# The low part of every other up-projection weight tile is formed by an adding transfer instead of a VectorE subtraction

## The chip, the cores and the metric

The kernel runs on one core of a Trainium2 chip. The core has TensorE (PE, with its weight loads as PEld), VectorE (DVE), ScalarE (ACT), GpSimd (POOL) and SyncE (SP), which only issues transfers here. Sixteen DMA engines move data between device memory and the on-chip memory. The metric is device time in microseconds (us) of one execution; lower is better.

## The reference, cut to what matters

One decoder layer over 256 tokens of width 2048: a normed residual goes through one q/k/v projection for two groups of heads (a softmax group and a stick-breaking group), each group's output is normed, one output projection and a residual follow, and then a squared-ReLU MLP of inner width 8192, a residual and a last norm. Everything is float32. The part that the change touches is the product with `w_up`:

```python
h = rmsnorm(x, mlp_norm_g[l])                       # (1, 256, 2048)
u = jnp.einsum('bsd,df->bsf', h, w_up[l])           # w_up: 2048 x 8192
x = x + jnp.einsum('bsf,fd->bsd', jnp.square(jax.nn.relu(u)), w_down[l])
return rmsnorm(x, final_norm_g)
```

## The kernel before, in words

**Items.** All weights (50.3 million float32 numbers, some 201 MB) are read once, as a stream of 1 MiB items (`items`, lines 81 to 97). An item is 512 rows by 512 columns, held as 128 partitions x 4 k-tiles x 512 columns. The stream is: 48 items of the q/k/v projection, 16 of the output projection ("o"), then twice 32 "up" items followed by 32 "down" items. An up item is named ("u", (half, c), j): c is one of 8 chunks of 512 columns in a half, and j = 0 to 3 is the quarter of the 2048 rows. So four items j = 0, 1, 2, 3 make one chunk, and there are 16 chunks.

**Two parts.** TensorE multiplies in the reduced format float32r. For float32 accuracy each item is split into a high part `wh` (the item rounded to float32r, ScalarE, `split_hi`, line 117) and a low part `wl` (item minus high part, VectorE, `split_lo`, line 123). The activations are split likewise. Each product is then high x high plus high x low plus low x high. In an up item (`w_stationary`, line 219) the weights are the stationary operand: for each of 4 column blocks m and 4 k-tiles, one matmul with `wh` over 512 columns (line 227: activations high and low side by side) is followed by one with `wl` over 256 columns (line 228). These 32 matmuls stand in a fixed order on TensorE, so the second matmul of an item is the first that needs `wl`.

**Order of the work.** The program is written out by hand; no scheduler moves it. `step` (line 268) handles item i: it issues the load of item i + 3 on SP, and it splits item i + 2 (`LOOK = 2`) while TensorE works on item i. The first half of the high part is issued ahead of the item's matmuls; in the middle of them come the second half of the high part and the first half of the low part, and after them the second half of the low part. Each engine runs its instructions in this order, and waits only for the semaphores of each. The tiles `raw`, `wh` and `wl` have three buffers each, so the parts of item i + 2 go where those of item i - 1 were.

**What stands between.** At the last quarter of a chunk (j = 3) each column block m is finished within the item, and `up_out` (line 467) turns it into `uT`: ScalarE copies the low accumulator (`ulow`, line 471), VectorE adds and squares (lines 472, 473), ScalarE writes the high part of `uT` (line 474), and GpSimd its low part (line 475). ScalarE waits in each of these four chains for VectorE. The split of the next chunk's j = 1 item stands in the same step, around and behind these chains. In the step of j = 1, where the j = 3 item is split, there are no such chains. GpSimd has nothing else in this stretch.

The other weights use the same split. In the down items (`x_stationary`, line 248) the activations are stationary and three matmuls of 512 columns are made for each k-tile and half of the tokens.

Of the kernel before, what the change touches and what calls it, by code (L numbers as in the profile page):

```python
# [9 lines left out]
F32 = mybir.dt.float32  # L10
F32R = mybir.dt.float32r
AF = mybir.ActivationFunctionType
ALU = mybir.AluOpType
AX = mybir.AxisListType

P = 128
# [12 lines left out]
KI = 4  # L29
WARM0, WARM1 = 12, 6  # L30
CW = 512


def shape_constants():
    """What depends on shapes alone: the rotary angles and the causal mask's fill."""
    inv = (THETA ** (-np.arange(HALF, dtype=np.float32) / HALF)).astype(np.float32)
    ang = np.arange(S, dtype=np.float32)[None, :] * inv[:, None]
    c, s = np.cos(ang, dtype=np.float32), np.sin(ang, dtype=np.float32)
    out = np.zeros((P, 2 * S + 3 * P), np.float32)
    out[:2 * HALF, :S] = np.concatenate([c, c])  # L40
    out[:2 * HALF, S:2 * S] = np.concatenate([-s, s])
    diag = np.where(np.arange(P)[None, :] <= np.arange(P)[:, None], 0.0, NEG)
    out[:, 2 * S:2 * S + P] = diag
    out[:, 2 * S + 2 * P:] = diag
    return out
# [3 lines left out]
def layer(ctx: ExitStack, tc, x, mix_g, w_in, moba_g, sb_g, w_out, mlp_g, w_up, w_down, fin_g,  # L49
          consts, out):  # L50
    nc = tc.nc
# [5 lines left out]
    att = pool("att", 2, space=bass.MemoryType.PSUM)  # L57
    ctx.enter_context(tc.manual_schedule())

    # ---- constants and small operands  # L60
    xs = cp.tile([P, 2, D], F32, name="xs")
    xv = x.rearrange("(t p) d -> p t d", p=P)
    grow = cp.tile([2 * HALF, P], F32, name="grow")
# [4 lines left out]
    def load_x(c):  # L68
# [7 lines left out]
                            fill=0.0, base=0, channel_multiplier=1)  # L76
    mhalf = cp.tile([P, 2], F32, name="mhalf")
    nc.gpsimd.memset(mhalf, -0.5)

    # ---- weight stream: 1 MiB items, each split exactly into two float32r parts  # L80
    items = []
    for h in range(2):
        for kind in ("q", "v", "k"):
# [13 lines left out]
            items += [("d", (hf, c), j, w_down, hf * 4096 + j * KI * P, c * CW) for j in range(8)]  # L97

    raws, parts = {}, {}

    def fetch(i):
        if i >= len(items):
# [16 lines left out]
    def split_lo(i, ks=slice(0, KI)):  # L119
        if i >= len(items):  # L120
            return
        wh, wl = parts[i]
        nc.vector.tensor_sub(wl[:, ks], raws[i][:, ks], wh[:, ks].bitcast(F32))  # L123

    def split_k(i, k, n=1):
        split_hi(i, slice(k, k + n))
        split_lo(i, slice(k, k + n))

    # ---- row statistics
    def rms_scale(r, ss, n):  # L130
        """r = (ss / n + eps) ** -0.5"""
        nc.vector.tensor_scalar(r, ss, 1.0 / n, EPS, op0=ALU.mult, op1=ALU.add)
        nc.gpsimd.tensor_tensor(r, r, mhalf[:, :r.shape[-1]], op=ALU.pow)

# [2 lines left out]
    actT = cp.tile([P, 16, 2 * S], F32R, name="actT")  # L137

    def to_columns(src, gcol, kts, between=None):
        """Transposes [token, d] into d on the partitions, times gain, in two parts."""  # L140
        ps = [att.tile([P, 512], F32, name="att") for _ in range(2)]
        for n, k in enumerate(kts):
            for t in range(2):
                c = n // 2 * S + t * P
                nc.tensor.transpose(ps[n % 2][:, c:c + P], src[:, t, k * P:(k + 1) * P], ident)  # L145
        for n, k in enumerate(kts):
            g = g48[:, gcol + k:gcol + k + 1]
            src_ps = ps[n % 2][:, n // 2 * S:(n // 2 + 1) * S]
            hi, lo = actT[:, k, 0:S], actT[:, k, S:2 * S]
            nc.scalar.activation(hi, src_ps, AF.Copy, scale=g)  # L150
            nc.vector.scalar_tensor_tensor(lo, src_ps, g, hi.bitcast(F32), op0=ALU.mult, op1=ALU.subtract)  # L151
            if between:
                between(n)
# [9 lines left out]
    r1b = cp.tile([P, S], F32, name="r1b")  # L163

    def x_piece(c, n):
        """A quarter of x, and the split of the weights that meet it, n of its tiles at a time."""
        def between(k):
            if k % 2:
                for j in range(k - 1, k + 1, n):
                    split_k(c, j, n)  # L170

        to_columns(xs, 0, list(range(4 * c, 4 * c + 4)), between)
# [3 lines left out]
            nc.scalar.activation(junk, xs[:, t, c * CW:(c + 1) * CW], AF.Square, accum_out=ss1[:, t, c:c + 1])  # L176

    def x_scale():
        """The first norm's row scale, along the tokens of every partition."""
        nc.vector.tensor_reduce(r1, ss1, axis=AX.X, op=ALU.add)  # L180
        rms_scale(r1, r1, D)
        for t in range(2):
            nc.vector.tensor_scalar(junk[:, t * P:(t + 1) * P], ident, r1[:, t:t + 1], None, op0=ALU.mult)
# [7 lines left out]
    idle = acc.tile([P, 512], F32, name="acc")  # L191

    def warm(n):
        """Products that nobody reads, for the array's clock to rise while the first loads run."""
        for _ in range(n):
            nc.tensor.transpose(idle[:, :P], ident, ident)

# [16 lines left out]
        nc.tensor.transpose(ps[:, :32], grow, ident[:32, :32])  # L214
        nc.vector.tensor_copy(g48[:, 16:48], ps[:, :32])

    # ---- products
    def w_stationary(i, ps, j, nj, done):
        """Columns of the weights on the partitions: [hi*hi | hi*lo + lo*hi]."""
        wh, wl = parts.pop(i)  # L220
        mk = [(m, k) for m in range(4) for k in range(KI)]
        if i < 3:
            mk = [(m, k) for k in range(KI) for m in range(4)]
        for n, (m, k) in enumerate(mk):
            kt = j * KI + k
            first, last = j == 0 and k == 0, j == nj - 1 and k == KI - 1
            nc.tensor.matmul(ps[m], wh[:, k, m * P:(m + 1) * P], actT[:, kt, :], start=first, stop=False)  # L227
            nc.tensor.matmul(ps[m][:, S:2 * S], wl[:, k, m * P:(m + 1) * P], actT[:, kt, 0:S],  # L228
                             start=False, stop=last)
            if last:  # L230
                done(m)
            if n == (3 if i < 3 else 7):
                yield

    def x_part(i, ps, j, nj, xT, k0, t, done):
        """Tokens on the partitions."""
        wh, wl = parts[i]
        for k in range(KI):
            kt = k0 + j * KI + k
            first, last = j == 0 and k == 0, j == nj - 1 and k == KI - 1  # L240
            hi, lo = xT[:, kt, t * P:(t + 1) * P], xT[:, kt, S + t * P:S + (t + 1) * P]
            nc.tensor.matmul(ps[t], hi, wh[:, k, :], start=first, stop=False)  # L242
            nc.tensor.matmul(ps[t], hi, wl[:, k, :], start=False, stop=False)  # L243
            nc.tensor.matmul(ps[t], lo, wh[:, k, :], start=False, stop=last)  # L244
        if last:
            done(t)
# [9 lines left out]
    hooks = {}  # L256

    def at(slot, f, *a):
        """Slots are half items: 2 * i in the middle of item i, 2 * i + 1 at its end."""
        hooks.setdefault(slot, []).append((f, a))  # L260

    def run_hooks(slot):
# [21 lines left out]
    for c in range(3):  # L284
        at(2 * c, x_piece, c + 1, 2)
    at(5, small_operands)
    for c in range(4):
        at((4, 5, 7, 9)[c], x_square, c)
# [1 line left out]
    at(10, x_scale)  # L290
    at(12, x_spread)

    # ---- attention
    with ExitStack() as phase:
        qkvp = phase.enter_context(tc.tile_pool(name="qkvp", bufs=2))
        aw = phase.enter_context(tc.tile_pool(name="aw", bufs=2))
# [3 lines left out]
        rg = op.tile([P, 2, 2], F32, name="rg")  # L300

        def qk_out(dst, ps, m):
            """Joins the two accumulators of a head."""
            low = aw.tile([P, S], F32, name="low")
            nc.scalar.copy(low, ps[:, S:2 * S])
            nc.vector.tensor_add(dst[:, m, :], ps[:, 0:S], low)

        def qk_scale(dst, m, rope):
            """Rotates the first 32 rows of a head, and applies the norm's scale."""
            if rope:  # L310
                rot = aw.tile([32, 2, S], F32, name="rot", bufs=1)
                nc.vector.stream_shuffle(rot[:, 0], dst[:32, m, :], [(r + HALF) % 32 for r in range(32)])
                nc.vector.tensor_mul(rot[:, 0], rot[:, 0], sinr)
                nc.vector.tensor_mul(rot[:, 1], dst[:32, m, :], cosr)
                nc.vector.tensor_add(dst[:32, m, :], rot[:, 0], rot[:, 1])
            nc.gpsimd.tensor_mul(dst[:, m, :], dst[:, m, :], r1b)
# [110 lines left out]
            if h == 1:  # L427
                at(i0 + 2 + gap * 3 + d2 + 2, group_scale, g)

        # ---- output projection and residual, one group after the other  # L430
        ssx = op.tile([P, 2, 4], F32, name="ssx")

        def o_out(g, c, ps, t):
# [25 lines left out]

    at(2 * state["i"] + 16, load_fgb)  # L460

    # ---- squared-ReLU MLP, in two halves of its inner width; relu(r u) ** 2 = r * r * relu(u) ** 2
    uT = mp.tile([P, 32, 2 * S], F32R, name="uT")
    ssf = mp.tile([P, 2, 4], F32, name="ssf")
    rf = mp.tile([P, 2], F32, name="rf")
# [23 lines left out]
                finish(t)  # L489

    def finish(t):
        """The last norm, in quarters that leave as they are ready."""
        r = rf[:, t:t + 1]
        nc.vector.scalar_tensor_tensor(r, ssf[:, t, 3:4], 1.0 / D, r, op0=ALU.mult, op1=ALU.add)
        nc.gpsimd.tensor_tensor(r, r, mhalf[:, :1], op=ALU.pow)
        for c in range(4):
            cs = slice(c * CW, (c + 1) * CW)
            o = xs[:, t, cs]
            if c % 2:
                if c == 3:  # L500
                    nc.vector.scalar_tensor_tensor(o, o, r, fgb[:, cs], op0=ALU.mult, op1=ALU.mult)
                else:
                    nc.scalar.activation(o, o, AF.Copy, scale=r)
                nc.scalar.dma_start(out[t * P:(t + 1) * P, cs], o)
            else:
                nc.vector.tensor_scalar(o, o, r, None, op0=ALU.mult)
                nc.sync.dma_start(out[t * P:(t + 1) * P, cs], o)
# [39 lines left out]
```

## Time and profile before

| what | value |
|---|---|
| time, median of 3 runs | 1113.27 us (1113.21 to 1113.61) |
| span of the profiled execution | 1111.6 us |
| time of the profiled execution itself | not listed apart from its span; the runs lie 1.6 to 2.0 us above that span |
| PE busy | 1099.6 us, 99% |
| DVE busy | 632.7 us, 57% |
| ACT busy | 505.7 us, 45% |
| POOL busy | 130.8 us, 12% |
| DMA | 207.96 MB, 187 GB/s over the span |

Busy time is the time in which an engine has at least one instruction at work; for TensorE, matmuls overlap, so the mean duration of one is longer than the distance from one to the next. An idle time in brackets stands ahead of the instruction in whose row it is, with what ended it. A transfer's time "to landing" is from its issue until its last byte has arrived.

### The profile page before, as it was taken

Reading aid. Unit: us, or ns where it says so; the run is one execution under the profiler, and the core shown is the slowest. Engines: PE = TensorE matmul, PEld = TensorE weight load, DVE = VectorE, ACT = ScalarE, POOL = GpSimd, SP = SyncE. Lnnn points to the kernel's source line nnn. Section 1 sums busy time; section 2 is a strip of 40 time slices with the busy share of each in tenths; the row PEclk is TensorE's granted clock in tenths of the full one; section 3 lists DMA queues with packets and bytes.
Section 4 is the critical chain, followed back from the end, with each engine's and each line's share of the span. In section 5 each row is a group of like instructions: output and inputs, shape, how many; then the busy total and the mean of one; then the engine's idle time right before and its main releaser. Section 6 shows DMA issues by size and latency. Waiting matters only on the chain.

```text
span 1111.6 us, 14050 instructions
## 1 busy us (share of the span) xinstructions
PE 1099.6 (99%) x5648; PEld 936.8 (84%) x5648; DVE 632.7 (57%) x813; ACT 505.7 (45%) x732; POOL 130.8 (12%) x154
## 2 busy tenths in 40 slices
PE   8999999999999999999999999999999999999997
PEld 7888888888888888888888888888888888888885
DVE  5655657668676665655564444435655665455453
ACT  5645444455444554544453333333544454334341
POOL 0101213223111001211220000000111211000000
PEclk9999999999999999999999999999999999999999
DMA  8655454554444555566546546554565456555542
GB/s 303 233 166 179 160 189 153 189 189 152 172 169 173 183 184 180 191 218 208 178 154 244 197 163 227 189 189 152 197 219 190 152 201 216 189 198 192 203 164 75
DMA packets 104113, 207.96 MB, mean 187 GB/s; under 512 B 3392, under 2 KB 3440, under 8 KB 103920
## 3 DMA queue, kind: packets, MB, share of 16 engines
q1 hardware_dynamic: 103088, 204.49, 53.8%
q10 hardware_dynamic: 960, 2.58, 0.6%
q8 instruction: 44, 0.72, 0.3%
q14 instruction: 21, 0.17, 0.0%
HBM read 204.96 MB, written 2.10 MB: 186 GB/s over the span
## 4 chain that ended last, share of the span: by engine, by line
PE 98%; DMA 1%; issue 1%; DVE 0%; ACT 0%; SPq 0%; POOLq 0%; POOL 0%; DVEq 0%
PE acc L227 32%; PE acc L228 16%; PE acc L242 16%; PE acc L244 16%; PE acc L243 16%; PE att L321 1%; PE att L372 1%; PE att L145 1%; DMA raw<-in_w_in 1%; PE att L362 0%; PE att L373 0%; PE att L320 0%; DVE wl L123 0%; DVE xs L479 0%; ACT junk L482 0%
## 5 line engine op out<-in xcount | busy, mean ns | idle before, releaser
L123 DVE TENSOR_TENSOR wl<-raw,wh 128x1024 fp32r<-128x1024 f32 (+1 forms) x386 | 461.2, 1231 | 197.6 <-ACT wh L117 197.6
L117 ACT ACTIVATE wh<-raw 128x1024 fp32r<-128x1024 f32 (+1 forms) x385 | 389.5, 1051 | 351.7 <-PE acc L244 199.0
L227 PE MATMUL acc<-actT,wh 128*128 128x512 f32 x1536 | 536.6, 393 | 0.6 <-DVE actT L151 0.6
L228 PE MATMUL acc<-actT,wl 128*128 128x256 f32 x1536 | 429.5, 280 | 0.2 <-DVE wl L123 0.2
L227 PEld LDWEIGHTS acc<-actT,wh 128*128 128x128 f32 x1536 | 288.4, 188 | 63.6 <-ACT wh L117 0.8
L228 PEld LDWEIGHTS acc<-actT,wl 128*128 128x128 f32 x1536 | 288.5, 188 | 0.9 <-DVE wl L123 0.5
L242 PE MATMUL acc<-wh,uT 128*128 128x512 f32 x512 | 199.2, 389 | 0.0
L244 PE MATMUL acc<-wh,uT 128*128 128x512 f32 x512 | 199.2, 389 | 0.0
L243 PE MATMUL acc<-wl,uT 128*128 128x512 f32 x512 | 199.2, 389 | 0.0
L475 POOL TENSOR_TENSOR uT<-u,uT 128x256 fp32r<-128x256 f32 x64 | 61.7, 964 | 510.6 <-ACT uT L474 510.6
L244 PEld LDWEIGHTS acc<-wh,uT 128*128 128x128 f32 x512 | 96.1, 188 | 20.1
L243 PEld LDWEIGHTS acc<-wl,uT 128*128 128x128 f32 x512 | 96.1, 188 | 20.0
L242 PEld LDWEIGHTS acc<-wh,uT 128*128 128x128 f32 x512 | 96.1, 188 | 19.7
L472 DVE TENSOR_TENSOR u<-acc,ulow 128x256 f32<-128x256 f32 x64 | 27.2, 425 | 100.0 <-ACT ulow L471 90.2
L474 ACT ACTIVATE uT<-u 128x256 fp32r<-128x256 f32 x64 | 26.8, 418 | 67.0 <-DVE u L473 67.0
L242 PE MATMUL acc<-wh,actT 128*128 128x512 f32 x128 | 53.1, 415 | 0.0
L242 PE MATMUL acc<-wh,oT 128*128 128x512 f32 x128 | 52.2, 408 | 0.0
L243 PE MATMUL acc<-wl,oT 128*128 128x512 f32 x128 | 50.5, 395 | 0.0
L244 PE MATMUL acc<-wh,oT 128*128 128x512 f32 x128 | 50.5, 394 | 0.0
L243 PE MATMUL acc<-wl,actT 128*128 128x512 f32 x128 | 50.4, 394 | 0.0
L244 PE MATMUL acc<-wh,actT 128*128 128x512 f32 x128 | 50.4, 394 | 0.0
L479 DVE SCALAR_TENSOR_TENSOR xs<-acc,r,xs 128x512 f32<-128x512 f32 x16 | 12.0, 750 | 45.3 <-PE acc L244 45.3
(105 smaller groups left out, 572.1 us busy)
## 6 DMA issues: line engine op xcount, KB each, us to landing
raw<-in_w_up SPq DMA_DIRECT2D x64, 1024.0 KB, 6.2
raw<-in_w_down SPq DMA_DIRECT2D x64, 1024.0 KB, 5.0
raw<-in_w_in SPq DMA_DIRECT2D x47, 1024.0 KB, 5.2
raw<-in_w_out SPq DMA_DIRECT2D x16, 1024.0 KB, 5.0
xs<-in_x SPq DMA_DIRECT2D x4, 512.0 KB, 9.6
raw<-in_w_in SPq DMA_DIRECT2D x4, 256.0 KB, 5.9
fgb<-in_final_norm_g ACTq DMA_DIRECT2D x1, 1024.0 KB
out<-xs SPq DMA_DIRECT2D x4, 256.0 KB, 3.2
```

The lines of the kernel that those rows point to most:

```text
L117: nc.scalar.activation(parts[i][0][:, ks], raws[i][:, ks], AF.Copy)
L123: nc.vector.tensor_sub(wl[:, ks], raws[i][:, ks], wh[:, ks].bitcast(F32))
L145: nc.tensor.transpose(ps[n % 2][:, c:c + P], src[:, t, k * P:(k + 1) * P], ident)
L227: nc.tensor.matmul(ps[m], wh[:, k, m * P:(m + 1) * P], actT[:, kt, :], start=first, stop=False)
L228: nc.tensor.matmul(ps[m][:, S:2 * S], wl[:, k, m * P:(m + 1) * P], actT[:, kt, 0:S], start=False, stop=last)
L242: nc.tensor.matmul(ps[t], hi, wh[:, k, :], start=first, stop=False)
L243: nc.tensor.matmul(ps[t], hi, wl[:, k, :], start=False, stop=False)
L244: nc.tensor.matmul(ps[t], lo, wh[:, k, :], start=False, stop=last)
L472: nc.vector.tensor_add(u, ps[:, 0:S], low)
L474: nc.scalar.activation(hi, u, AF.Copy)
L475: nc.gpsimd.tensor_sub(lo, u, hi.bitcast(F32))
L479: nc.vector.scalar_tensor_tensor(xs[:, t, cs], ps[t], r2[:, t:t + 1], xs[:, t, cs], op0=ALU.mult, op1=ALU.add)
```

## The change

For the up items with odd j (two in each chunk, 32 in all), `split_lo` no longer subtracts on VectorE. ScalarE writes minus the high part into `wl`, in two halves at the places where the two subtractions stood. Behind the second half GpSimd issues one transfer that reads the whole item once more from device memory and adds it onto `wl` in its place. All other items are split as before. Of the 64 up items 32 are so changed; no other engine's order is altered, apart from the two subtractions that VectorE loses for each. (Line numbers after the diff are larger: 117 becomes 121, 123 becomes 134, 471 to 475 become 482 to 486; the new lines are 128 and 131.)

```diff
+    def by_queue(i):
+
+        return items[i][0] == "u" and items[i][2] % 2 == 1
+
...
     def split_lo(i, ks=slice(0, KI)):
         if i >= len(items):
             return
         wh, wl = parts[i]
+        if by_queue(i):
+            nc.scalar.activation(wl[:, ks], wh[:, ks].bitcast(F32), AF.Copy, scale=-1.0)
+            if ks.stop == KI:
+                _, _, _, w, k0, c0 = items[i]
+                nc.gpsimd.dma_start(wl, w[k0:k0 + KI * P, c0:c0 + CW].rearrange("(k p) c -> p k c", p=P),
+                                    accum_op=ALU.add)
+            return
         nc.vector.tensor_sub(wl[:, ks], raws[i][:, ks], wh[:, ks].bitcast(F32))
```

On ScalarE, in the step of a chunk's last quarter (j = 3), the order before is this; `wh_3756` is the high part of the next chunk's j = 1 item, `wh_3828` that of its j = 2 item:

```order
L471 COPY ulow_3767<-acc_3630 128x256
L474 ACTIVATE uT_3417<-u_3768 128x256
L471 COPY ulow_3782<-acc_3631 128x256
L474 ACTIVATE uT_3417<-u_3783 128x256
L117 ACTIVATE wh_3756<-raw_3714 128x1024
L471 COPY ulow_3799<-acc_3632 128x256
L474 ACTIVATE uT_3417<-u_3800 128x256
L471 COPY ulow_3814<-acc_3633 128x256
L474 ACTIVATE uT_3417<-u_3815 128x256
L117 ACTIVATE wh_3828<-raw_3754 128x1024
```

ScalarE in the same place with the change (`wh_3760` and `wl_3761` are the parts of the j = 1 item, `wh_3833` belongs to j = 2):

```order
L482 COPY ulow_3771<-acc_3633 128x256
L485 ACTIVATE uT_3418<-u_3772 128x256
L482 COPY ulow_3786<-acc_3634 128x256
L485 ACTIVATE uT_3418<-u_3787 128x256
L121 ACTIVATE wh_3760<-raw_3718 128x1024
L128 ACTIVATE wl_3761<-wh_3760 128x1024
L482 COPY ulow_3803<-acc_3635 128x256
L485 ACTIVATE uT_3418<-u_3804 128x256
L482 COPY ulow_3818<-acc_3636 128x256
L485 ACTIVATE uT_3418<-u_3819 128x256
L128 ACTIVATE wl_3761<-wh_3760 128x1024
L121 ACTIVATE wh_3833<-raw_3758 128x1024
```

Two negated copies have come in, the second behind the last of the four chains.

On GpSimd, over one chunk and its neighbours with the change (`wl_3761` is that j = 1 item, `wl_3875` the j = 3 item of the same chunk); before, only the rows of `uT` stood here:

```order
L131 DMA wl_3567<-in_w_up 128x4x512
L131 DMA wl_3680<-in_w_up 128x4x512
L486 TENSOR_TENSOR uT_3418<-u_3772,uT_3418 128x256
L486 TENSOR_TENSOR uT_3418<-u_3787,uT_3418 128x256
L486 TENSOR_TENSOR uT_3418<-u_3804,uT_3418 128x256
L486 TENSOR_TENSOR uT_3418<-u_3819,uT_3418 128x256
L131 DMA wl_3761<-in_w_up 128x4x512
L131 DMA wl_3875<-in_w_up 128x4x512
```

The transfer of a j = 1 item stands behind the four low parts of `uT` of the chunk before, and that of the j = 3 item directly behind it.

## Rows read from the trace of the kernel before

**Rows 1.** The page: span, and busy time of engines (share, instructions).
```profile
span 1111.6 us, 14050 instructions
...
PE 1099.6 (99%) x5648; PEld 936.8 (84%) x5648; DVE 632.7 (57%) x813; ACT 505.7 (45%) x732; POOL 130.8 (12%) x154
```

**Rows 2.** The page: chain of work that ended last, shares by engine.
```profile
PE 98%; DMA 1%; issue 1%; DVE 0%; ACT 0%; SPq 0%; POOLq 0%; POOL 0%; DVEq 0%
```

**Rows 3.** The page: costliest groups, lines 123 and 117 (busy us, mean ns | idle before).
```profile
L123 DVE TENSOR_TENSOR wl<-raw,wh 128x1024 fp32r<-128x1024 f32 (+1 forms) x386 | 461.2, 1231 | 197.6 <-ACT wh L117 197.6
L117 ACT ACTIVATE wh<-raw 128x1024 fp32r<-128x1024 f32 (+1 forms) x385 | 389.5, 1051 | 351.7 <-PE acc L244 199.0
```

**Rows 4.** Timeline of ACT, one chunk's last quarter (start us, us, instruction, idle before).
```profile
549.79 1.06 ACT L117 ACTIVATE wh<-raw 128x1024 fp32r<-128x1024 f32 x1 [3.49 <-PE acc L227]
551.29 0.38 ACT L471 COPY ulow<-acc 128x256 f32<-128x256 f32 x1 [0.44 <-PE acc L228]
...
554.71 1.05 ACT L117 ACTIVATE wh<-raw 128x1024 fp32r<-128x1024 f32 x1
...
558.74 0.42 ACT L474 ACTIVATE uT<-u 128x256 fp32r<-128x256 f32 x1 [1.02 <-DVE u L473]
559.06 3.89 ACT L117 ACTIVATE wh<-raw 128x1024 fp32r<-128x1024 f32 x4
...
571.98 1.06 ACT L117 ACTIVATE wh<-raw 128x1024 fp32r<-128x1024 f32 x1 [3.49 <-PE acc L227]
```

**Rows 5.** Timeline of PE, two neighbouring high products and the low one between.
```profile
560.80 0.39 PE L227 MATMUL acc<-actT,wh 128*128 128x512 f32 x1
561.03 0.28 PE L228 MATMUL acc<-actT,wl 128*128 128x256 f32 x1
561.15 0.39 PE L227 MATMUL acc<-actT,wh 128*128 128x512 f32 x1
```

**Rows 6.** Timeline of POOL, last low part of `uT` in that chunk.
```profile
559.23 1.21 POOL L475 TENSOR_TENSOR uT<-u,uT 128x256 fp32r<-128x256 f32 x1 [0.95 <-ACT uT L474]
```

**Rows 7.** Timeline of ACT, around the first chunk of each half.
```profile
401.99 1.04 ACT L117 ACTIVATE wh<-raw 128x1024 fp32r<-128x1024 f32 x1
...
411.17 2.01 ACT L117 ACTIVATE wh<-raw 128x1024 fp32r<-128x1024 f32 x2 [3.51 <-PE acc L227]
...
746.33 2.01 ACT L117 ACTIVATE wh<-raw 128x1024 fp32r<-128x1024 f32 x2 [3.43 <-PE acc L244]
...
757.21 2.01 ACT L117 ACTIVATE wh<-raw 128x1024 fp32r<-128x1024 f32 x2 [3.43 <-PE acc L227]
```

**Rows 8.** Line 110, all weight loads: time from issue to landing.
```profile
DMA to landing us min/median/max: 4.9/5.4/10.1
```

**Rows 9.** Windows, busy us (x) by engine, PEclk, DMA share, GB/s: start, up stretch.
```profile
10.00:20.00 10.00, 9.58 (x61) 8.69 (x62) 6.31 (x11) 5.87 (x12) 0.00 (x0) 1.00 1.06 387
480.00:555.00 75.00, 75.00 (x435) 66.05 (x434) 42.01 (x55) 34.68 (x54) 12.60 (x14) 1.00 0.56 190
```

**Rows 10.** Windows at the program's end, PEclk third from the right.
```profile
1102.00:1104.00 2.00, 1.32 (x6) 0.75 (x4) 0.64 (x1) 0.00 (x0) 0.00 (x0) 1.00 1.04 386
...
1106.00:1107.00 1.00, 0.00 (x0) 0.00 (x0) 1.00 (x3) 0.45 (x1) 0.00 (x0) 1.00 0.00 0
1107.00:1108.00 1.00, 0.00 (x0) 0.00 (x0) 0.27 (x1) 0.00 (x0) 0.00 (x0) 0.50 0.93 348
```

**Rows 11.** Timeline of PE: the first twelve transposes, and eight later ones.
```profile
1.51 2.82 PE L196 MATMUL acc<-ident 128*128 128x128 f32 x12 [1.51 <-POOL mhalf L78]
...
16.88 1.03 PE L145 MATMUL att<-ident,xs 128*128 128x128 f32 x8
```

## The prediction
> **What bounds the kernel now.** I read the page's busy times first: TensorE is busy for 1099.6 of 1111.6 us, GpSimd for an eighth of it [rows 1]. The chain of work that ended last confirms it: 98% of it is TensorE, and VectorE and ScalarE have 0% [rows 2]. So time can only be added or taken where TensorE waits, and VectorE's relief alone is worth nothing. I then read the timeline of one chunk of the up-projection, since the change lies there: what matters is how long before its first use each low part is ready. ScalarE's copies at 549.79 and 571.98 stand at the same place of two successive chunks [rows 4], so a chunk lasts 22.19 us and an item 5.55 us. TensorE alternates high and low products without a gap, and the low one begins 0.23 us after the high one [rows 5]. So an item's low part is needed 0.23 us after TensorE enters the item.
>
> The profiled execution's own time is known by its span alone, 1111.6 us. The median of the runs, 1113.3, lies 1.7 above; I add up on the span and put 1.7 on at the end.
>
> **What goes.** 64 subtractions of 1.23 us on VectorE [rows 3], 79 us of busy time that lies beside TensorE's work. Gain: nothing.
>
> **What comes, item j = 1.** It is split in the step of the previous chunk's j = 3, which ScalarE enters at 549.79. Between the two halves of the high part stand two output chains and behind them two more; ScalarE leaves the last at 559.06 and goes on at once [rows 4], so here it is behind, not ahead. The two negated copies have the shape of a split copy, 1.05 us, one starting 0.97 us after another (3.89 us for four) [rows 4]. The first delays the last two chains by 0.97, the second then starts at 559.06 + 0.97 = 560.03 and ends at 561.08. TensorE enters the j = 1 item two items after the j = 3 one: 549.79 + 11.10 = 560.89, and its first low product is due at 561.12. So the negated high part is complete at the very moment at which the finished low part is due. GpSimd's own last piece of the chunk, 1.21 us from 559.23 [rows 6], moves 0.97 back and ends at 561.4: the transfer can go about 0.3 later still. Let L be the time from then until it has landed. TensorE waits for L, to some tenths, at every ordinary chunk boundary. Behind the waiting low product stands all of TensorE's queue; nothing passes it.
>
> **How long is L?** The trace has no transfer issued by GpSimd and none that adds. The nearest rows are the plain loads of the same 1 MiB: 4.9 us at least, 5.4 as median, 10.1 at most [rows 8]. At the 387 GB/s that the engines moved when they were full [rows 9], 1 MiB takes 2.7, so some 2.2 of 4.9 are fixed. An adding transfer must read the item and the present content of the tile. If both go through the same engines, the data part is 5.4. Ordinary loads go on beside it: the up stretch moves 190 GB/s on average [rows 9], and after ScalarE's copies at this point up to two loads (another 5.4) can be released; I charge half, 2.7. GpSimd has to prepare the transfer, of 512 pieces of 2 KB; an instruction of its own takes 1.2 [rows 6], and I charge that. L = 2.2 + 5.4 + 2.7 + 1.2 = 11.5 us. Ends: 4.9, the cheapest plain load, and 20.2, twice the slowest one.
>
> The Trainium skill, "Collectives: The Full Stack", section "The bandwidth ceiling: the fold count and why AG ≠ RS ≠ AR", says that a reducing transfer is half as fast as a copy because each chunk needs two source reads through the same ring. No run here shows it; it speaks for the doubled data part, and without that part the wait would be 2.7 shorter per chunk. By the skill's "DMA: Bandwidth & Descriptors", section "Anatomy of one DMA — SWDGE (gpsimd) path", a transfer issued by GpSimd takes 2.0 us and its bytes at 436 GB/s: 4.4 us for a plain MiB, 6.8 with both reads. That estimate, with nothing beside it, would make the sum 14 x 4.7 = 66 us smaller.
>
> **Item j = 3.** Its split stands in the step of j = 1, without output chains. ScalarE gets there after the second copy above: the two copies for j = 2, two for j = 3 and two negated ones, 6 x 0.97 from 561.08, end at 566.9. The item is due two items after j = 1 is entered, plus j = 1's own wait: 560.89 + 11.10 + 0.23 + L = 572.2 + L. So this transfer has 5.3 us more than the first; j = 1's wait hides it. It costs nothing unless it takes 5.3 longer than the first; each us beyond that costs up to 16 us in all. The j = 2 item, split by ScalarE by 563.0 and by VectorE 2.4 later, is due at 566.7 + L and is safe.
>
> **Two chunks differ.** The first of all is split while the output projection ends. ScalarE's copy at 401.99 is where the second negated copy comes in, which so ends at 403.04; j = 2 is entered at 411.17 [rows 7], j = 1 one item before, at 405.6, due at 405.8. Wait: L - 2.8 = 8.7. The first chunk of the second half is split in the last down item, entered at 746.33, with no chains: two copies and two negated ones end at 750.3, and j = 1 is entered at 757.21 [rows 7], due at 757.4. Wait: L - 7.1 = 4.4.
>
> Sum of waits: 14 x 11.5 + 8.7 + 4.4 = 174 us.
>
> **The clock.** TensorE's last matmul begins shortly before 1103.3 and it is idle from there (1.32 us busy of the window from 1102). The granted clock still reads 1.00 until 1107 and 0.50, which is 1.2 of 2.4 GHz, from then on [rows 10]. So an idle time of 3.7 us had lowered it, and a wait of 11.5 will. What it costs until the clock is back no row shows. Ends: nothing, and one whole item at half pace, 5.5. The nearest row is the program's beginning, where twelve transposes take 2.82 us and eight later ones 1.03 [rows 11]: at the later pace twelve take 1.5, a loss of 1.3, though the granted clock is not told of there. I take 2 us for each of 16 waits, 32 us.
>
> The Trainium skill, "TensorE: Matmul & The Clock Gate", section "HAM oscillation — how this bites in real kernels", tells of a loop whose every tile starts at half clock since the transfer's wait ahead of it has lowered it. The fall at 1107 agrees; that it comes at each of 16 waits no run here shows yet. Without the rule the sum is 174, with it 206.
>
> 1111.6 + 174 + 32 + 1.7 = **1319 us**, say 1320.
>
> **The rivals.**
> *Cheap transfer.* The addition costs no more than a load: L = 5.4. For it: the engines are busy for only 56% of the up stretch [rows 9]. Against: two reads, and GpSimd's preparation. Waits 14 x 5.4 + 2.6 = 78, clock between 0 and 30: 1191 to 1222 us.
> *Slow transfer.* The addition runs far below a load's pace, or GpSimd is slow with 512 pieces. L = 18: 14 x 18 + 15.2 + 10.9 = 278, clock 32: 1423 us. If the j = 3 transfer, issued 5.8 after the first, has to queue behind it, its own wait comes on top, 16 us for each us: up to 1500.
> *Not slower.* The one way: the transfer lands before TensorE gets to the low product. The place is the chunk boundary, the price is then zero (1113 us), and the point that decides is whether ScalarE finishes the second negated copy at least 4.9 us, the shortest landing of any MiB [rows 8], before 561.1. For it: at the second half's first chunk it does so by 7.1. Against: in 14 chunks ScalarE's chains, each with 1.02 us of waiting for VectorE [rows 4], fix its end at 561.08, and TensorE would have to be 5 us late for another reason.
>
> **How the numbers follow.** My forecast (L from 8 to 16; 1260 to 1395 us) has 0.55, the cheap transfer 0.17 (with what lies between it and the forecast), the slow one 0.24, not slower 0.03; 0.01 is left over. The likeliest gives 1320. The range of 8 in 10 runs from 1205, where the cheap case begins to have its clock loss, to 1450, into the slow case. A change within 0.2% (2.2 us) can't be told from none. Faster by more than that has 0.01, within it 0.02, slower 0.97.
>
> **What would show it.** Right: low products of the up stretch (old line 228) named as waiting for GpSimd's transfer into `wl`, 16 large idle times on TensorE of 8 to 16 us and none at j = 3; granted clock under 1 behind them; VectorE 79 us less busy, ScalarE 67 more; 34 MB more read; q/k/v, output and down stretches unchanged. Wrong: 32 waits (then j = 3 isn't hidden); waits of 5 us (the transfer is as cheap as a load) or 18; no fall of the clock after waits above 4 us; or TensorE's lost time standing at a high product, where a late load or copy would be the cause.

## Result, and the profile after

| | before | with the change |
|---|---|---|
| time, median | 1113.44 us (1113.21 to 1113.81, 4 runs) | 1291.43 us (1290.18 to 1293.12, 4 runs) |
| span of the profiled execution | 1111.6 us | 1291.4 us |
| granted TensorE clock, mean | 0.998 | 0.938 |

The ratio is 1.16, with a 95% interval of 1.1584 to 1.1616: 178 us slower. The forecast was 1320 us. Times in the tables are medians, and one run of e7 below, at 1174.15 us and in a slower state, is left out of its median.

The page of the changed kernel first: span, busy times, and the chain that ended last.

```profile
span 1291.4 us, 14149 instructions
...
PE 1137.0 (88%) x5648; PEld 964.0 (75%) x5648; DVE 558.2 (43%) x749; ACT 565.6 (44%) x796; POOL 159.8 (12%) x186
...
PE 75%; DMA 12%; ACT 4%; issue 3%; DVE 3%; POOL 2%; POOLq 0%; DVEq 0%; ACTq 0%
```

TensorE fell from 99% to 88% [rows 1] and from 98% to 75% of the chain [rows 2]. VectorE is 74.5 us less busy and ScalarE 59.9 more, and neither decides anything by itself. The costliest groups say where TensorE waits:

```profile
L239 PE MATMUL acc<-actT,wl 128*128 128x256 f32 x1536 | 446.4, 291 | 143.5 <-DMA wl<-in_w_up 143.5
...
L134 DVE TENSOR_TENSOR wl<-raw,wh 128x1024 fp32r<-128x1024 f32 (+1 forms) x322 | 384.1, 1229 | 414.1 <-ACT wh L121 414.1
...
L131 POOL DMA_DIRECT2D wl<-in_w_up x32 | 41.5, 1297 | 292.0 <-ACT wl L128 251.1
L128 ACT ACTIVATE wl<-wh 128x1024 fp32r<-128x1024 f32 x64 | 65.0, 1041 | 0.0
```

The low products (line 239, before 228) stand idle for 143.5 us, all of it until the adding transfer has landed; 64 subtractions are gone from VectorE [rows 3]. One chunk boundary shows how. ScalarE's timeline, in the place of [rows 4]:

```profile
535.90 0.42 ACT L485 ACTIVATE uT<-u 128x256 fp32r<-128x256 f32 x1 [1.02 <-DVE u L484]
536.22 1.04 ACT L128 ACTIVATE wl<-wh 128x1024 fp32r<-128x1024 f32 x1
537.17 3.88 ACT L121 ACTIVATE wh<-raw 128x1024 fp32r<-128x1024 f32 x4
540.96 1.99 ACT L128 ACTIVATE wl<-wh 128x1024 fp32r<-128x1024 f32 x2
```

GpSimd's in the same stretch, in the place of [rows 6]:

```profile
536.39 0.74 POOL L486 TENSOR_TENSOR uT<-u,uT 128x256 fp32r<-128x256 f32 x1 [0.95 <-ACT uT L485]
537.57 1.30 POOL L131 DMA_DIRECT2D wl<-in_w_up  x1 [0.43 <-ACT wl L128]
543.24 1.28 POOL L131 DMA_DIRECT2D wl<-in_w_up  x1 [4.38 <-ACT wl L128]
```

And TensorE's, in the place of [rows 5]:

```profile
536.91 0.28 PE L239 MATMUL acc<-actT,wl 128*128 128x256 f32 x1
537.03 0.39 PE L238 MATMUL acc<-actT,wh 128*128 128x512 f32 x1
546.71 0.55 PE L239 MATMUL acc<-actT,wl 128*128 128x256 f32 x1 [9.29 <-DMA wl<-in_w_up]
547.06 0.63 PE L238 MATMUL acc<-actT,wh 128*128 128x512 f32 x1
547.49 0.41 PE L239 MATMUL acc<-actT,wl 128*128 128x256 f32 x1
```

The second negated copy ends at 537.26; the first low product of the j = 1 item would have begun at 537.26 too (0.23 behind the high one). It begins at 546.71. Behind it the pairs come every 0.64 us (the next high product is at 547.71) instead of every 0.35. Windows around the boundary before that one, in the columns of [rows 10], show why; TensorE has stopped at 503.4 and goes on at 512.96:

```profile
506.00:507.00 1.00, 0.00 (x0) 0.00 (x0) 0.58 (x1) 1.00 (x3) 0.00 (x0) 1.00 1.04 164
507.00:508.00 1.00, 0.00 (x0) 0.00 (x0) 0.00 (x0) 1.00 (x3) 0.00 (x0) 0.57 1.09 184
508.00:513.00 5.00, 0.04 (x1) 0.07 (x1) 0.00 (x0) 0.92 (x1) 1.28 (x1) 0.50 1.08 252
513.00:517.00 4.00, 4.00 (x13) 3.42 (x14) 0.00 (x0) 0.00 (x0) 0.00 (x0) 0.50 1.08 290
518.00:520.00 2.00, 2.00 (x14) 1.75 (x13) 0.00 (x0) 0.00 (x0) 0.00 (x0) 1.00 1.09 259
```

The granted clock falls to 1.2 GHz in the wait, is still there for the first 4 us of work, and then returns to 2.4 GHz. The transfers, first the queues (packets, MB, share of 16 engines' span), then the issues (KB each, median us to landing), then the landings of line 131:

```profile
q1 hardware_dynamic: 103088, 204.49, 46.7%
q0 software_dynamic: 16896, 33.56, 14.7%
...
raw<-in_w_up SPq DMA_DIRECT2D x64, 1024.0 KB, 8.8
...
wl<-in_w_up POOLq DMA_DIRECT2D x32, 1024.0 KB, 9.9
...
DMA to landing us min/median/max: 8.4/9.9/14.9
```

The median of 9.9 lies between two groups: the j = 1 transfers of the 14 ordinary chunks take 9.0 to 9.4 us and the j = 3 transfers behind them 13.8 to 14.9. Per packet the adding queue takes 0.147 x 1291.4 us x 16 / 16896 = 180 ns, the loads 0.467 x 1291.4 x 16 / 103088 = 94 ns. The plain loads of this stretch now land after 8.8 us, against 6.2 before.

Whether loads share the engines with a j = 1 transfer shows at the boundary of the windows above, where it is issued at 503.54. First the window behind its issue, in the columns of [rows 10], and then the only queue that moves packets from 505.6 to 510 (packets, MB, share of the engines):

```profile
503.54:505.50 1.96, 0.00 (x0) 0.00 (x0) 1.28 (x2) 1.96 (x3) 1.30 (x1) 1.00 0.00 0
```
```profile
q0 software_dynamic: 384, 0.79, 108.5%
```

For 2.0 us nothing moves; then the adding transfer has the engines to itself, and keeps them busy, for at least three quarters of its MiB.

### The profile page after: what moved, and what is told of

Its sections match the earlier page's. It is cut to its first block, busy times and chain, and to the rows that moved or that the text cites. A ratio compares the mean times of both kernels' runs of the same rounds, so it can differ in the third digit from the quotient of the medians.

```text
span 1291.4 us, 14149 instructions
## 1 busy us (share of the span) xinstructions
PE 1137.0 (88%) x5648; PEld 964.0 (75%) x5648; DVE 558.2 (43%) x749; ACT 565.6 (44%) x796; POOL 159.8 (12%) x186
## 3 DMA queue, kind: packets, MB, share of 16 engines
q1 hardware_dynamic: 103088, 204.49, 46.7%
q0 software_dynamic: 16896, 33.56, 14.7%
## 4 chain that ended last, share of the span: by engine, by line
PE 75%; DMA 12%; ACT 4%; issue 3%; DVE 3%; POOL 2%; POOLq 0%; DVEq 0%; ACTq 0%
PE acc L238 21%; PE acc L253 14%; PE acc L255 13%; PE acc L254 13%; DMA wl<-in_w_up 11%; PE acc L239 11%; POOL uT L486 2%; DVE u L484 1%; DVE u L483 1%; ACT wh L121 1%; ACT wl L128 1%; ACT uT L485 1%; ACT ulow L482 1%; PE att L156 1%; PE att L332 1%
## 5 line engine op out<-in xcount | busy, mean ns | idle before, releaser
L239 PE MATMUL acc<-actT,wl 128*128 128x256 f32 x1536 | 446.4, 291 | 143.5 <-DMA wl<-in_w_up 143.5
L238 PE MATMUL acc<-actT,wh 128*128 128x512 f32 x1536 | 565.8, 409 | 0.0
L134 DVE TENSOR_TENSOR wl<-raw,wh 128x1024 fp32r<-128x1024 f32 (+1 forms) x322 | 384.1, 1229 | 414.1 <-ACT wh L121 414.1
L239 PEld LDWEIGHTS acc<-actT,wl 128*128 128x128 f32 x1536 | 304.6, 198 | 149.4 <-issue 145.0
L238 PEld LDWEIGHTS acc<-actT,wh 128*128 128x128 f32 x1536 | 303.9, 198 | 67.9 <-ACT wh L121 0.2
L486 POOL TENSOR_TENSOR uT<-u,uT 128x256 fp32r<-128x256 f32 x64 | 49.2, 769 | 368.8 <-ACT uT L485 368.8
L131 POOL DMA_DIRECT2D wl<-in_w_up x32 | 41.5, 1297 | 292.0 <-ACT wl L128 251.1
L128 ACT ACTIVATE wl<-wh 128x1024 fp32r<-128x1024 f32 x64 | 65.0, 1041 | 0.0
L253 PE MATMUL acc<-wh,actT 128*128 128x512 f32 x128 | 53.1, 415 | 0.0
```

The costliest lines, as they stand in the source:

```text
L128: nc.scalar.activation(wl[:, ks], wh[:, ks].bitcast(F32), AF.Copy, scale=-1.0)
L131: nc.gpsimd.dma_start(wl, w[k0:k0 + KI * P, c0:c0 + CW].rearrange("(k p) c -> p k c", p=P), accum_op=ALU.add)
L486: nc.gpsimd.tensor_sub(lo, u, hi.bitcast(F32))
```

## Experiments

Each ran beside the kernel before (medians 1113.2 to 1113.4 us). Diffs are against the changed kernel and are cut to what matters; "..." marks lines left out.

| experiment | us | ratio to before, 95% |
|---|---|---|
| e1, j = 1 only | 1289.06 | 1.1565 to 1.1599 |
| e2, j = 3 only | 1246.23 | 1.1176 to 1.1213 |
| e3, transfers that nobody reads | 1146.99 | 1.0287 to 1.0317 |
| e4, split early in the step | 1224.44 | 1.0932 to 1.1044 |
| e5, one read instead of two | 1239.85 | 1.1119 to 1.1152 |
| e6, busy in the wait | 1274.42 | 1.1427 to 1.1461 |
| e7, e2 with half of the up loads | 1156.82 | 1.0363 to 1.0414 |
| e8, e3 without transfers | 1113.47 | 0.9991 to 1.0010 |
| e9, j = 1 only, hidden | 1114.88 | 1.0005 to 1.0024 |
| e10, the change with half of the up loads | 1290.77 | 1.1572 to 1.1611 |
| e11, e3 with half of the up loads | 1113.61 | 0.9992 to 1.0012 |
| e12, e1, busy in the wait | 1272.37 | 1.1412 to 1.1461 |

**e1 and e2: one kind of item alone.**

```diff
-        return items[i][0] == "u" and items[i][2] % 2 == 1
+        return items[i][0] == "u" and items[i][2] == 1        # e2: == 3
```

> Only the j = 1 items (16) take their low part from the adding transfer; the j = 3 items are split as before. Theory A (time is lost only where TensorE waits for the j = 1 transfer, 14 waits of some 9.5 us and two shorter ones, and about 2 us of low clock behind each; j = 3 is hidden by that wait): 1285 to 1293 us, 16 waits. Theory B (each of the 32 transfers costs its share, by contention or by ScalarE's and GpSimd's extra work): about half of the loss, near 1200 us.

> Only the j = 3 items (16) take their low part from the adding transfer. Theory A: without the wait at j = 1 the j = 3 item loses its cover. ScalarE ends its second negated copy about 565.0 on the clock of the rows of before, the transfer lands some 9.5 us later, and the low part is due at 572.2: 16 waits of 1.5 to 3 us, too short to lower the clock; 1135 to 1160 us, granted clock near 1.00. Theory B: near 1200 us. If the j = 3 transfer were harmless by itself: 1113 to 1116 us.

e1 gave 1289.06: the j = 1 items account for 175.8 of the 178 us, and the j = 3 items add only some 2 beside them. e2 was a miss: 133 us, not 22 to 47. Alone, the j = 3 transfer is far from harmless. GpSimd's row and TensorE's next wait in e2 (the transfer's issue, then the low product that it releases):

```profile
532.88 1.30 POOL L131 DMA_DIRECT2D wl<-in_w_up  x1 [4.96 <-ACT wl L128]
```
```profile
546.38 0.55 PE L239 MATMUL acc<-actT,wl 128*128 128x256 f32 x1 [6.29 <-DMA wl<-in_w_up]
```

It lands after 13.4 us (median of the 16: 13.3), not 9.5. The last readers of two `raw` tiles, VectorE's subtraction for j = 2 and ScalarE's copy for j = 3, end at 530.1 and 530.7, and two loads are issued right then, ahead of the transfer. From 533 to 537.4 the engines move nothing but loads:

```profile
q1 hardware_dynamic: 773, 1.55, 102.2%
```

The wait is 6.3 us, and the product behind it takes 0.55: the clock had fallen too. This gave the second theory, A2: the transfer and the loads share the DMA engines, and what it meets depends on where it is issued.

**e3, e8, e11: the work without the wait.** `sh` is a tile that no product reads; VectorE subtracts as before. e8 leaves out the transfer, e11 the loads of odd items.

```diff
-        if by_queue(i):
-            nc.scalar.activation(wl[:, ks], wh[:, ks].bitcast(F32), AF.Copy, scale=-1.0)
+        if by_queue(i) and shadow:                  # j == 1 only
+            sh = shadow[0]
+            nc.scalar.activation(sh[:, ks], wh[:, ks].bitcast(F32), AF.Copy, scale=-1.0)
...
-                nc.gpsimd.dma_start(wl, w[k0:k0 + KI * P, ...
+                nc.gpsimd.dma_start(sh, w[k0:k0 + KI * P, ...
-            return
```

> 15 of the j = 1 items make the negated copies and the adding transfer in full, but into a tile that no product reads; their low part is subtracted on VectorE as before. That tile takes the place of the last norm's gain, whose load and factor are left out (the factor is replaced by another tile). Theory A: the same copies, bytes and GpSimd work cost nothing when nobody waits for them: 1112 to 1118 us, granted clock 1.00. Theory B (contention with the loads, or ScalarE's delay of the output chains): 1140 us or more, against e1.

> As e3 (negated copies into a tile that no product reads, VectorE subtracts as before), but without the transfer. Theory A2 (e3 lost its 33 us because the transfers hold up the ordinary loads, not because of ScalarE's copies): 1112 to 1116 us. If ScalarE's copies delay the output chains or the next splits enough: 1130 us or more.

> As e3 (15 adding transfers into a tile that no product reads), with the loads of the up items with odd j left out (their high part is made from the item before). Theory A2 (e3 lost 33 us because the transfers and the loads share the DMA engines and the high parts came late): nothing is lost, 1112 to 1116 us. If the unread transfer costs something by itself: 1130 us or more.

e3 was a miss: 33.7 us are lost with nobody waiting for the transfer. The waits of ScalarE's splits for loads say where, in e3 first and then before (us in total, times, longest us):

```profile
ACT wh L121 <- DMA raw<-in_w_up: 88.5, 20, 6.6
```
```profile
ACT wh L117 <- DMA raw<-in_w_up: 5.3, 1, 5.3
```

The loads came late, so high parts and then low parts came late. TensorE stands idle for 21.3 us before VectorE's low parts, and its busy time is 11.3 us longer, at a mean clock of 0.992. e8 and e11 show that it takes both: with the copies but no transfer nothing is lost, and with the transfers but half of the loads nothing either. So 15 adding transfers do no harm by themselves; together with the full loads, and issued at this place, they do (e9 below issues them at another).

**e4: the split early in the step.**

```diff
+        early = ahead < len(items) and by_queue(ahead)
         if i > LOOK:
             split_hi(ahead, h0)
+        if early:
+            split_hi(ahead, h1)
+            split_lo(ahead, h0)
+            split_lo(ahead, h1)
         for _ in work(i):
             run_hooks(2 * i)
-            split_hi(ahead, h1 if i > LOOK else slice(0, KI))
-            split_lo(ahead, h0)
+            if not early:
+                split_hi(ahead, h1 if i > LOOK else slice(0, KI))
+                split_lo(ahead, h0)
...
```

> Both kinds of items as in the change, but all four pieces of their split (two high, two negated) stand ahead of the matmuls of the step, so that for j = 1 ScalarE issues them before the output chains, about 7.3 us earlier. Theory A: the j = 1 wait falls from 9.6 to 2 to 3 us, the clock stays at 1.00, and j = 3, with less cover, waits 0 to 2 us: 1140 to 1180 us. Theory B (the place on ScalarE does not matter): 1280 us or more.

The direction held and the size did not: 67 us better than the change, 111 worse than before. TensorE's first three waits of the up stretch, with GpSimd's issue of the transfer that ends the third:

```profile
409.24 0.55 PE L239 MATMUL acc<-actT,wl 128*128 128x256 f32 x1 [3.38 <-DMA wl<-in_w_up]
436.05 0.39 PE L239 MATMUL acc<-actT,wl 128*128 128x256 f32 x1 [1.53 <-DMA wl<-in_w_up]
453.04 0.55 PE L239 MATMUL acc<-actT,wl 128*128 128x256 f32 x1 [5.61 <-DMA wl<-in_w_up]
```
```profile
439.58 1.30 POOL L131 DMA_DIRECT2D wl<-in_w_up  x1 [5.16 <-ACT wl L128]
```

The first two are j = 1 items, the third is a j = 3 item: the transfer issued at 439.58 is the second of its chunk. Of the 18 waits (69.5 us in all) only three stand at j = 1, of 1.5 to 3.4 us; the other 15 stand at j = 3, 12 of them of 3.7 to 5.9 us. So the earlier place does to j = 1 what was expected, and a little more: behind a j = 3 wait the next j = 1 item of the same half does not wait at all, since that wait gives its transfer time. What failed is the part on j = 3, for which 0 to 2 us were expected: its transfers take 9.2 to 13.3 us and have lost their cover. After 3.38 us of idleness the next product took 0.55, after 1.53 it took 0.39, and behind the 12 longer waits 0.55. So most of the remaining waits still cost a clock fall (mean clock 0.967), which the expectation had left out. The length of a wait alone does not settle this: in e2 one of 3.38 us, too, was followed by a product of 0.36.

**e5: one read.**

```diff
-                nc.gpsimd.dma_start(wl, w[...].rearrange("(k p) c -> p k c", p=P), accum_op=ALU.add)
+                nc.gpsimd.dma_start(wl, w[...].rearrange("(k p) c -> p k c", p=P))
```

> The change, but GpSimd's transfer only writes the item over the tile and adds nothing, so it has one read instead of two (the low part of these items is then the whole weight). In the run of the change the transfer's packets took 180 ns on an engine against 94 for a load's, and 5.5 us of 9.2 are data. Theory A (two reads set the length): the transfer lands 2.5 to 3 us sooner, the wait at j = 1 falls from 9.5 to some 6.7, the clock still falls: 1240 to 1258 us. Theory B (GpSimd's preparation and fixed time set it): 1280 us or more.

1239.85, just under the lower edge of the first. The page's queue row of e5, and one chunk boundary, GpSimd's issue and TensorE's first low product:

```profile
q0 software_dynamic: 16896, 33.56, 9.3%
```
```profile
522.66 0.79 POOL L131 DMA_DIRECT2D wl<-in_w_up  x1 [0.43 <-ACT wl L128]
528.55 0.55 PE L238 MATMUL acc<-actT,wl 128*128 128x256 f32 x1 [6.04 <-DMA wl<-in_w_up]
```

A packet now takes 0.093 x 1235.7 x 16 / 16896 = 109 ns, against 180. At the ordinary chunk boundaries the transfer lands after 5.7 to 6.0 us, against 9.0 to 9.4, and the waits are 6.0 to 6.5. GpSimd's own instruction is shorter too, 0.79 us against 1.30. So adding costs 3.0 to 3.7 us per MiB over writing, most of it in the packets: 33 on each engine, 71 ns longer, are 2.3 us. Whether the second read or the addition itself makes a packet longer, e5 does not separate. (The expectation's 5.5 us of data was too low: in the change the packets of such a transfer run for 6.6 to 7.0 us.)

**e6 and e12: TensorE busy in the wait.** In e12 only the j = 1 items take the transfer.

```diff
+    NWARM = 85
...
             nc.tensor.matmul(ps[m], wh[:, k, m * P:(m + 1) * P], actT[:, kt, :], start=first, stop=False)
+            if n == 0 and by_queue(i) and items[i][2] == 1 and items[i][1][1] > 0:
+                warm(NWARM, att.tile([P, 512], F32, name="att"))
```

> The change, with 85 transposes that nobody reads behind the first high product of each j = 1 item (14 chunks, not the first of a half), so that TensorE is busy for some 8.5 to 9 us of the 9.5 us wait. Theory A (behind each wait the clock is low for some 4 us, which costs 2.0 us): the transfer lands as before and the clock stays at 1.00, about 28 us less: 1260 to 1266 us. If the clock cost nothing beside the wait: 1291 us.

> As e1 (only j = 1 by the adding transfer) with the 85 transposes of e6 in the wait. In e6 17 us came back where 14 x 2.0 = 28 were due. If the rest was eaten by the j = 3 transfer, which with a shorter chunk runs closer to the next loads and transfer, then without it the full 28 come back: 1259 to 1264 us. If the transposes themselves overrun the wait (9.4 us and the product behind them) or the clock costs less than 2.0 us: 1270 us or more.

Both missed by the same amount: 17 us came back in each, not 28. TensorE's rows in e6:

```profile
503.06 9.44 PE L209 MATMUL att<-ident 128*128 128x128 f32 x85
513.08 0.36 PE L243 MATMUL acc<-actT,wl 128*128 128x256 f32 x1 [0.58 <-DMA wl<-in_w_up]
```

Here the first low product takes 0.36 us instead of 0.55, and the mean clock is 0.995: the cold stretch is gone. But waits of 0.4 to 2.2 us are left behind the transposes, since the transfer lands later than without them (median 9.7 in e12, 9.2 in e1). The j = 3 transfer isn't the reason, as e12 shows. Nor are the start or the loads: in e1 and in e12 the first packet moves 2.0 to 2.3 us after the issue, and the next loads come 7.0 to 7.3 us after it. It is the packets themselves. In the 3.5 us from the first packet on, the adding queue moves 0.57 to 0.64 MB in the 14 chunks of e1 and 0.51 to 0.58 in those of e12. One transfer of e1 (from 505.64), one of e12 (from 506.58), and one of e9 (from 490.64; its queue row alone):

```profile
q0 software_dynamic: 279, 0.57, 105.3%
```
```profile
q0 software_dynamic: 257, 0.53, 104.6%
```
```profile
q0 software_dynamic: 294, 0.60, 102.9%
```

In e9 TensorE is busy with matmuls throughout this stretch, and the transfer is no slower than in e1, where TensorE is idle. So it is not a busy TensorE as such, but the 85 transposes beside which the packets take longer; why, no run tells.

**e7 and e10: half of the up loads.**

```diff
     def fetch(i):
...
+        if items[i][0] == "u" and items[i][2] % 2 == 1:
+            raws[i] = raws[i - 1]
+            return
```

> As e2 (only j = 3 by the adding transfer), but the items with odd j are not loaded: their high part is made from the item before, so half of the loads of the up stretch are left out (and these items' weights are wrong). In e2 the transfer took 13.3 us, with two loads released just ahead of it. Theory A2 (it shares the DMA engines with them, and alone it takes 9 to 9.5): the wait falls from 6.3 to 2 to 2.7 us, too short to lower the clock: 1145 to 1160 us. If the transfer is as slow there for another reason: 1240 us or more.

> The change, with the loads of the items with odd j left out (their high part is made from the item before, so their weights are wrong). It says how much of the 9.2 us of the j = 1 transfer is sharing with the loads, for which the prediction charged 2.7 us. If only some tenths are (at j = 1 the loads come behind the transfer): 1278 to 1288 us. If 2.7 are: 1255 us or less.

e7: 1156.82, and the transfer lands after a median of 8.6 us, against 13.3 in e2; the waits are 1.5 to 2.2 us and once 3.8. So meeting the two loads was worth 4.7 us there, and 89 us in all. e10: no gain at all, 1290.77. TensorE's waits for the transfer in e10, beside 143.5 in the change:

```profile
PE acc L242 <- DMA wl<-in_w_up: 141.3, 17, 10.1
```

At the chunk boundary the transfer meets hardly a load, as the queue row from 505.6 to 510 showed; the loads that ScalarE's copies free there come behind it.

**e9: the j = 1 transfer hidden.** As e1 and e4 together, and in these items all high products ahead of the low ones:

```diff
...
+            if by_queue(i) and items[i][2] == 1:
+                lows.append((m, k, kt, last))
+                if n == 15:
+                    for m, k, kt, last in lows:
+                        nc.tensor.matmul(ps[m][:, S:2 * S], wl[:, k, m * P:(m + 1) * P], actT[:, kt, 0:S],
+                                         start=False, stop=last)
+            else:
...
```

> Only the j = 1 items by the adding transfer, split at the beginning of the step as in e4 (transfer some 7 us earlier), and in these items TensorE makes all 16 high products before the 16 low ones, which puts the first low product 3.5 us later. Theory A2 (what is lost is the wait for the transfer; when that is hidden, what remains is that it holds up the ordinary loads, 33 us in e3): waits for the transfer of 0 to 1 us, clock 1.00, 1115 to 1150 us. If the transfer's work itself costs TensorE time: above 1200 us.

1114.88 us, 1.0014 of before and just under the lower edge of the forecast. TensorE waits for no transfer of line 131, and the adding transfers land as soon as in e7:

```profile
wl<-in_w_up POOLq DMA_DIRECT2D x16, 1024.0 KB, 8.6
```

The same 16 transfers cost 176 us in e1 and 1.6 here. What is lost is not their work but the place at which their result is due. Of the 33 us that e3 lost to late loads nothing is left either: no split waits for a load of `w_up` here (88.5 us in e3), and hardly a load runs beside the transfers, so that loss belongs to the place as well. Whether it goes because the transfer is issued earlier, or because the early split frees its `raw` tile earlier, e9 does not separate. The version gains nothing on the kernel before, as VectorE's relief can't: TensorE is 99% busy in both.

## Why the prediction was right, and where its sizes were off

**Where the time goes** was right: at the j = 1 item's first low product, in all 14 ordinary chunks, with ScalarE's second negated copy ending (537.26) when the low part is due. e9, which moves when the item is split, and so when the transfer is issued, and when its result is used, takes the loss away.

**The length L** was 11.5 and is some 9.2 (e1: 9.1 to 9.4 in the ordinary chunks). Of its four terms, the one charged for sharing with loads, 2.7 us, is the one that failed: at the boundary shown the engines move nothing but the transfer for at least three quarters of its bytes, and e10, with half of the loads, waits as long. Where a transfer meets hardly a load at all (e7, e9) it lands after 8.6, so the sharing is worth some 0.6. The other terms came out within a us: from the issue to the first packet and from the last packet to the landing pass 2.0 and 0.4 us, for which 2.2 fixed and 1.2 of preparation were charged (GpSimd's instruction took 1.30), and the data part was 6.2 in e7 and e9, for which 5.4 was charged. The added cost of adding held: e5, without it, lands 3.0 to 3.7 us sooner, for which 2.7 was charged. The Trainium skill's rule ("Collectives: The Full Stack", section "The bandwidth ceiling: the fold count and why AG ≠ RS ≠ AR"), that two source reads halve the rate, agrees roughly with the packets: 180 ns against 94 of the loads, and against 109 of the same queue without the addition (e5), which is a factor of 1.65. The page states it for the reducing step of a collective, and no run here tells the second read from the addition. The 14 waits are 134.6 us in place of 161 (143.5 less the other three).

**The two special chunks** waited 5.9 and 1.6 us, for 8.7 and 4.4; each is 2.8 short, with landings of 8.9 and 8.4. Where the wait was 1.6, the j = 3 item behind it waited too:

```profile
862.35 0.36 PE L239 MATMUL acc<-actT,wl 128*128 128x256 f32 x1 [1.47 <-DMA wl<-in_w_up]
```

The prediction had no wait at j = 3, and its condition, a landing 5.3 us later than the first one's, does not cover this one: the transfer took 10.4 us, only 1.9 more than the first, but it was issued at 851.85, 9.0 us before its use. The 5.3 us hold for the ordinary chunks alone.

**Item j = 3** cost nothing beside j = 1 in the ordinary chunks, as forecast: e1 against the change, 2.4 us in all. Its transfer took up to 14.9 us, 5.7 more than the first; the item had 5.3, and some 2 more that the low clock adds (at the boundary shown it landed 2.4 us before its use). But its price without a cover was mis-sized: e2's expectation, counted as in the prediction, put 1.5 to 3 us on each wait, and e2 shows 6.3, and 133 us in all, since this transfer, unlike the first, does meet two loads. The sharing that was charged to j = 1 belongs to j = 3.

**The clock** was right: 32 us forecast. TensorE's busy time, for the same 5648 matmuls, grew from 1099.6 [rows 1] to 1137.0, by 37.4 us; behind 15 of the 17 waits the first product takes 0.55 us, so a fall costs some 2.5 where 2 were charged. The Trainium skill's account ("TensorE: Matmul & The Clock Gate", section "HAM oscillation — how this bites in real kernels") of a loop that goes cold at every transfer's wait agrees for the waits of 5.9 us and more; behind the two of 1.6 and 1.5 us the first product takes 0.36.

**The rivals.** The cheap transfer is refuted by e5: adding costs at least 3 us per MiB. The slow one would need landings of 18; the slowest was 14.9. "Not slower" needed the result 5 us ahead of its use; e9 gives it 7 us by the split's place and 3.5 by the products' order (both as its expectation reckoned them), and it is then not slower. The 4.9 us of the prediction would not have been enough: in the second half's first chunk the transfer was issued 7.0 us before its result was due, and TensorE still waited 1.6.

**Open:** why the adding transfer's packets are slower beside the transposes (e6, e12). In e12 its landings are 0.9 us later on average in the 14 chunks, some 12 us, which is about what the expectation missed.

## What to carry to other kernels

Moving work from an engine with slack to a transfer pays nothing if the path is elsewhere, and costs the transfer's whole latency, here 9.2 us, if it is issued where its result is due: count from the instruction that releases the transfer to the product that reads it. A wait of this kind costs more than its length: some 2.5 us each for the clock here. What a transfer meets on the DMA engines depends on which buffers are freed just ahead of it (8.6 or 13.3 us for the same MiB), so it must be priced at its own place. And a wait can cover the next transfer: taking one away can bring another out, as in e2 and e4.

## What was not expected of the hardware

- An adding transfer from device memory onto on-chip memory moves a MiB at about the half of a load's rate (180 ns for a 2 KB packet against 94), which the prediction had charged; that it slows the loads around it was not charged: in the up stretch they land after 8.8 us instead of 6.2, and in e3 that cost 33.7 us.
- GpSimd's subtraction for `uT` became faster, 769 ns on average against 964. Before, its pieces took 0.75 us and 1.15 to 1.21 in turn, the longer ones each beside a VectorE subtraction; with the change 60 of 64 took 0.73 to 0.75, and the four beside which VectorE still subtracts, in the last chunk of each half, took 1.15 to 1.21.
- An adding transfer lands later beside 85 transposes on TensorE (e12): 9.7 against 9.2 us as median, up to 11.3 against 9.4. Beside TensorE's matmuls (e9) it does not.
